# Seven block products for the keys and queries of seven head pairs, on normalized input

## The chip, the cores and the metric

The kernel runs on one core of a Trainium2 chip. The metric is the device time of one execution in microseconds (us): the median of several runs. TensorE (PE) multiplies, VectorE (DVE), ScalarE (ACT) and GpSimd (POOL) work elementwise, SyncE (SP) issues most transfers.

## What is computed

One step of a small encoder trunk: 512 prompt frames and 8 streams of 16 sample frames, 640 columns in all, 1024 features. A convolution module and an FFN come first, then one attention layer with an FFN, then a final norm. The change lies in the attention layer:

```python
k, v = jnp.split(rms_norm(h, norm_kv) @ w_kv, 2, axis=-1)
q = (rms_norm(h, norm_attn[j]) @ w_q[j]).reshape(B, T, N_HEADS, HEAD_DIM)
...
o = band_attention_prompt(q, k, v, rel_bias[j])
h = h + o @ w_o[j]
```

`rms_norm` divides a frame by its root mean square and multiplies by a gain per feature. There are 16 heads of 64, worked on as 8 pairs; the prompt attends within itself, the samples to 512 cached rows and their own.

## The kernel before

Features lie on partitions (8 tiles of 128), frames on the free axis. Every matrix product is made in three: each operand is split into a high part (a rounded copy, made by ScalarE) and a low part (the rest, a subtraction on VectorE), and high x high, low x high and high x low are added up in PSUM. So a weight tile costs a ScalarE and a VectorE operation before TensorE may use it.

The stage begins where the first layer's FFN ends. The FFN's last products are made for group 0 (256 columns) and then for group 1 (384 columns), eight output tiles each, and VectorE adds them into h (L705).

`rms_late` (L314) splits the raw h for each group (L190, L192) and works out 1/rms beside that: squares on ScalarE (L211), their sum over the eight tiles (L233), a product with a column of ones on TensorE for the mean (L243), epsilon on VectorE (L280), the power on Pool (L287) and a product that spreads the result over the partitions (L257). The row of 1/rms is used only at the eviction of a projection: L1228 and L1310 multiply keys and queries by it, L1251 and L1338 the values. The gains are multiplied into the weights when these are split: L167 and L168 (`wsplit`) for pair 0, L1290 and L1291 (`pieces`) for the others, in 16 pieces of 128 columns.

`run(proj_kq(0), proj_v(0))` makes the first pair's keys and queries and the first values: keys and queries of group 0, values of group 0, then the same of group 1. After that comes the loop over the pairs. A pair's attention is the steps A (scores of two heads, row maxima, exponentials, normalisation), S (sample scores), B and T (transposes), C (products with the values), written in `BO`. Between the steps, portions f of other products fill TensorE: `stream()` yields the projections of later pairs (k), values (v) and output products (o) in the order of `SETS`, and `FILL` says how many portions a pair takes. In `set_kq` (L1296) a pair's keys and queries are four results (two groups, two kinds) of 8 x 3 matmuls each, of 256 or 384 columns. The weights of the next set are split while the current set runs, in whole tiles of 2048 columns with two buffers. `samp_load` fetches a pair's cached keys and values when the pair begins.

A scheduler puts the instructions in the order of each engine, and each engine works through its own in that order. `high_priority` moves instructions ahead, `behind` and `issue_after` hold them back.

Of the kernel before, what the change touches and what calls it, by code (L numbers as in the profile page):

```python
# [8 lines left out]
F32 = mybir.dt.float32  # L9
# [6 lines left out]
P = 128  # L16
# [49 lines left out]
BO = ["A f4 S w f4 B f3 T f3 C f*"] * 8  # L66
BO[1] = BO[6] = "A f4 S w f5 B f5 T f5 C"
BO[7] = "A f2 S f2 w f4 B f3 T f3 C f*"
FILL = 20, 19, 28, 27, 28, 20, 19, 16
SETS = "k1 v1 k2 k3 o0 k4 v2 k5 o1 k6 v3 k7 o2"  # L70
# [15 lines left out]
def tile_trunk(ctx, tc, xT, vecs, hist, w_pw1, w_pw2, w_in0, w_out0, w_os0, w_in1, w_out1, w_os1,  # L86
# [227 lines left out]
    def rms_late(g, gain, engs=SQ, cut=CUT):  # L314
        n = gr[g][1]
        xh, xl = new_xs(g)
        for k in range(KT):
            src = hp(g, k)
            if gain is not None:
                t = tp.tile([P, tw[0]], F32, tag="n1", name=nm("n1"), bufs=NB1)  # L320
                nc.vector.tensor_scalar(out=t[:, :n], in0=src, scalar1=col(gain, k),
                                        scalar2=None, op0=ALU.mult)
                src = t[:, :n]
# [787 lines left out]
    tps, early = ExitStack(), ExitStack()  # L1111
    op_ = early.enter_context(tc.tile_pool(name="op", bufs=1, reuse_waits="tile"))
    xp = early.enter_context(tc.tile_pool(name="xp1", bufs=1, reuse_waits="tile"))
    w2 = early.enter_context(tc.tile_pool(name="w2c", bufs=2, space=PSUM, reuse_waits="tile"))
    mm = tps.enter_context(tc.tile_pool(name="mm3", bufs=4, space=PSUM, reuse_waits="tile"))
    tp = tps.enter_context(tc.tile_pool(name="tp2", bufs=2, reuse_waits="tile"))

    xs = [rms_late(0, None), rms_late(1, None)]
    tps.close()
    at = ExitStack()  # L1120
    am = at.enter_context(tc.tile_pool(name="am", bufs=2, space=PSUM))
    mm = at.enter_context(tc.tile_pool(name="mm1", bufs=2, space=PSUM))
# [173 lines left out]
    def set_kq(p, w):  # L1296
# [4 lines left out]
        for g, (g0, n) in enumerate(GR):  # L1301
            for t, dst in enumerate((kt, qt)):
                pt = mmt()
                for a, b in zip(PARTS, PARTS[1:]):
# [3 lines left out]
                    if b == KT:  # L1308
# [9 lines left out]
                        if g and t:  # L1318
                            nc.sync.dma_start(k_out[p], kt)
                            split[p] = heads_split(p)  # L1320
# [516 lines left out]
```

## Time and profile before

| | |
|---|---|
| median of 3 runs | 1445.13 us (1444.21 to 1446.97) |
| the profiled execution | 1444.19 us |
| its span | 1442.4 us |
| TensorE busy | 1419.1 us, 98% |
| VectorE, ScalarE, Pool busy | 77%, 52%, 20% |
| the FFN's last product ends, first projection begins | 663.8, 664.7 us |
| first attention step | 692.2 us |
| data moved | 192.57 MB, mean 134 GB/s |

The profile is one execution. A busy share says how full an engine is, not whether something waits for it; here TensorE is full nearly everywhere, and the question at each place is which other engine it would wait for. A row of the timeline has start, duration, engine, line, operation, output<-inputs and count; in brackets stands the idle time before it and what ended it. Durations of matmuls overlap.

### The profile page before, as it was taken

Reading aid. Unit: us, or ns where it says so; the run is one execution under the profiler, and the core shown is the slowest. Engines: PE = TensorE matmul, PEld = TensorE weight load, DVE = VectorE, ACT = ScalarE, POOL = GpSimd, SP = SyncE. Lnnn points to the kernel's source line nnn. Section 1 sums busy time; section 2 is a strip of 40 time slices with the busy share of each in tenths; the row PEclk is TensorE's granted clock in tenths of the full one; section 3 lists DMA queues with packets and bytes.
Section 4 is the critical chain, followed back from the end, with each engine's and each line's share of the span. In section 5 each row is a group of like instructions: output and inputs, shape, how many; then the busy total and the mean of one; then the engine's idle time right before and its main releaser. Section 6 shows DMA issues by size and latency. Waiting matters only on the chain. (4 is left out here: it accounts for less than half of the span.)

```text
span 1442.4 us, 28233 instructions
## 1 busy us (share of the span) xinstructions
PE 1419.1 (98%) x11086; PEld 1366.2 (95%) x11086; DVE 1114.5 (77%) x2474; ACT 746.0 (52%) x1617; POOL 282.9 (20%) x335
## 2 busy tenths in 40 slices
PE   9999999999999999999999999998999999999998
PEld 8998799999999999999998999988999999999998
DVE  6789867898788789766666757667898788888855
ACT  5666554564554554545654544534564554554443
POOL 5789121011111111012111111110011111111101
PEclk9999999999999999999999999999999999999999
DMA  7267424054534445424456455561034544444512
GB/s 246 74 185 182 131 81 143 13 142 125 156 95 141 132 116 127 139 88 172 164 185 219 166 179 183 182 207 60 30 106 123 160 113 121 130 119 124 148 59 74
DMA packets 66932, 192.57 MB, mean 134 GB/s; under 512 B 12144, under 2 KB 30320, under 8 KB 58480
## 3 DMA queue, kind: packets, MB, share of 16 engines
q1 hardware_dynamic: 52432, 160.58, 34.0%
q0 software_dynamic: 13504, 29.37, 10.2%
q8 instruction: 87, 1.43, 0.4%
q10 hardware_dynamic: 864, 0.83, 0.2%
q14 instruction: 45, 0.37, 0.1%
HBM read 179.14 MB, written 11.61 MB: 132 GB/s over the span
## 5 line engine op out<-in xcount | busy, mean ns | idle before, releaser
L442 PE MATMUL mm<-XH,whi 128*128 128x320 f32 x896 | 275.7, 310 | 2.6 <-ACT t L454 2.6
L442 PE MATMUL mm<-XH,wlo 128*128 128x320 f32 x896 | 276.1, 309 | 0.0
L442 PE MATMUL mm<-XL,whi 128*128 128x320 f32 x896 | 274.5, 309 | 0.0
L374 ACT ACTIVATE whi<-raw 128x512 fp32r<-128x512 f32 (+2 forms) x280 | 168.8, 613 | 136.0 <-PE mm L442 105.5
L375 DVE TENSOR_TENSOR wlo<-raw,whi 128x512 fp32r<-128x512 f32 (+2 forms) x280 | 184.2, 666 | 17.4 <-ACT whi L374 16.2
L442 PE MATMUL mm<-hid,whi 128*128 128x320 f32 x732 | 171.8, 310 | 3.0 <-DVE hid L375 2.2
L442 PEld LDWEIGHTS mm<-XH,whi 128*128 128x128 f32 x896 | 167.7, 188 | 4.2 <-ACT t L454 4.2
L442 PEld LDWEIGHTS mm<-XH,wlo 128*128 128x128 f32 x896 | 168.1, 188 | 0.0
L442 PEld LDWEIGHTS mm<-XL,whi 128*128 128x128 f32 x896 | 167.7, 188 | 0.0
L442 PEld LDWEIGHTS mm<-hid,whi 128*128 128x128 f32 x732 | 124.8, 188 | 5.5 <-DVE hid L375 3.2
L202 PE MATMUL mm<-xh,whi 128*128 128x320 f32 (+2 forms) x416 | 129.0, 312 | 0.8 <-DVE h L705 0.4
L203 PE MATMUL mm<-xh,wlo 128*128 128x320 f32 (+2 forms) x416 | 127.9, 309 | 0.0
L204 PE MATMUL mm<-xl,whi 128*128 128x320 f32 (+2 forms) x416 | 125.8, 310 | 0.0
L442 PE MATMUL mm<-hid,wlo 128*128 128x320 f32 x366 | 113.0, 309 | 0.0
L442 PE MATMUL mm<-XH,shi 128*128 128x320 f32 x344 | 105.9, 309 | 0.7 <-DVE h L1552 0.7
L442 PE MATMUL mm<-XH,slo 128*128 128x320 f32 x344 | 106.0, 308 | 0.0
L442 PE MATMUL mm<-XL,shi 128*128 128x320 f32 x344 | 105.5, 308 | 0.0
L420 POOL DMA_DIRECT2D s<-in_w_in x38 | 22.1, 581 | 372.7 <-DVE wlo L375 147.7
L844 POOL TENSOR_TENSOR ca<-ca,cvt 128x512 f32<-128x512 f32 x60 | 91.8, 1530 | 16.4 <-ACT cvt L841 9.9
L374 ACT ACTIVATE shi<-raw 128x512 fp32r<-128x512 f32 (+1 forms) x114 | 66.7, 588 | 44.7 <-PE mm L442 41.2
L454 ACT ACTIVATE t<-mm 128x320 f32<-128x320 f32 x114 | 49.5, 434 | 64.5 <-PE mm L442 64.2
L583 DVE TENSOR_TENSOR h<-h,mm 128x320 f32<-128x320 f32 x168 | 79.6, 479 | 2.9 <-PE mm L442 2.8
(330 smaller groups left out, 3673.7 us busy)
## 6 DMA issues: line engine op xcount, KB each, us to landing
raw<-in_w_in SPq DMA_DIRECT2D x38, 1024.0 KB
s<-in_w_in POOLq DMA_DIRECT2D x76, 256.0 KB, 4.1
raw<-in_w_os SPq DMA_DIRECT2D x24, 768.0 KB
cache<-in_ck SPq DMA_DIRECT2D x32, 512.0 KB
cache<-in_cv SPq DMA_DIRECT2D x32, 512.0 KB
raw<-in_w_pw SPq DMA_DIRECT2D x11, 1024.0 KB
s<-in_w_os POOLq DMA_DIRECT2D x48, 192.0 KB, 3.6
raw<-in_w_kq SPq DMA_DIRECT2D x8, 1024.0 KB
```

The costliest lines, as they stand in the source:

```text
L202: nc.tensor.matmul(ps, wh, xh, start=(first and i == 0), stop=False)
L203: nc.tensor.matmul(ps, wl, xh, start=False, stop=False)
L204: end = nc.tensor.matmul(ps, wh, xl, start=False, stop=(stop and i == last))
L374: put_end[1] = nc.scalar.activation(out=hi, in_=src, func=AF.Copy).ins
L375: put_end[0] = nc.vector.tensor_tensor(out=lo, in0=src, in1=hi.bitcast(F32), op=sub).ins
L420: nc.gpsimd.dma_start(s1, src[:, 2 * n:3 * n])
L442: last = nc.tensor.matmul(pt, wt, v, start=(first and k == i == 0), stop=(k == n - 1 and i == 2), skip_group_check=True)
L454: keeps.append(nc.scalar.activation(out=t, in_=pt, func=AF.Copy).ins)
L583: nc.vector.tensor_tensor(out=hv, in0=hv, in1=pt, op=sub if row else add)
L844: nc.gpsimd.tensor_tensor(out=acc, in0=acc, in1=pr, op=ALU.add)
```

## The change

- **Seven products.** The keys and queries of pairs 1 to 7 are a product of a 2 x 2 block matrix of weights (keys and queries by two halves of the features) with a 2 x 2 block matrix of input (halves of the features by halves of the columns). It is made with seven block products of 4 x 3 matmuls of 320 columns instead of eight. The block sums of the input (`xsum`, four with high and low parts) are made once by VectorE and ScalarE, those of the weights for each pair by VectorE. The seven products alternate between two PSUM banks and are evicted by copies on ScalarE and additions on VectorE.
- **Normalized input.** The sums need input that has been divided by its rms. `rms_kept` (in place of `rms_late`) works out 1/rms first, multiplies h by it on VectorE (L324 of the new kernel) and splits the product (L192, L194). The evictions become plain copies. The squares lie in two tiles, the sum in a third, for both groups.
- **Gains.** For keys and queries ScalarE multiplies the raw weights by the gains in place, 16 pieces of 128 columns, and the blocks are then added and split in seven pieces of 512 columns.
- **A ring.** Split weights lie in six slots of 512 columns; `advance` makes pieces up to nine portions ahead, if a slot is free. Raw weights come in quarters into one buffer. The second buffers of before hold cached keys and values now, which are fetched in two steps: values after S, the next pair's keys after C.
- **Order.** `SETS`, `BO` and `FILL` are new: v1 comes before k1, and a keys-and-queries set has 14 portions of 6 matmuls instead of 12 of 6 or 9. The scores, transposes and products of the attention are as before.

```diff
-SETS = "k1 v1 k2 k3 o0 k4 v2 k5 o1 k6 v3 k7 o2"
-FILL = 20, 19, 28, 27, 28, 20, 19, 16
+FILL = 29, 21, 26, 26, 24, 24, 25, 16
+LEAD = 9
+RING = 6
+SETS = "v1 k1 k2 v2 k3 o0 k4 k5 o1 k6 v3 k7 o2 o3"
...
-    def rms_late(g, gain, engs=SQ, cut=CUT):
-        n = gr[g][1]
-        xh, xl = new_xs(g)
-        for k in range(KT):
-            src = hp(g, k)
...
-            xsplit(src, xh[:, k, :], xl[:, k, :])
-        rt = cst.tile([P, 4], F32, tag=f"rt{g}", name=nm("rt"))
+    def rms_kept(g, x, rows, sqs, acc):
+        g0, n = gr[g]
+        xh, xl = (t[:, :, g0:g0 + n] for t in x)
         with tc.high_priority(offset=HP):
-            bc, _ = rstd_bc([hp(g, k) for k in range(KT)], n, engs, cut, rt,
-                            nc.vector if g else nc.gpsimd)
-        b = xp.tile([P, n], F32, tag=f"bc{g}", name=nm("bc"))
-        nc.scalar.activation(out=b, in_=bc, func=AF.Copy)
-        return xh, xl, b, rt
+            bc, _ = rstd_bc([hp(g, k) for k in range(KT)], n, SQ, CUT, None, nc.vector, accp=acc,
+                            sqs=sqs)
+            for k in range(KT):
+                t = rows[k][:, g0:g0 + n]
+                nc.vector.tensor_tensor(out=t, in0=hp(g, k), in1=bc, op=ALU.mult)
+                xsplit(t, xh[:, k, :], xl[:, k, :])
+        return xh, xl
...
-    xs = [rms_late(0, None), rms_late(1, None)]
+    for g in range(2):
+        q = [kept[:, i, :gr[g][1]] for i in range(3)]
+        xs.append(rms_kept(g, xall, rows, (q[0], q[1]) * 4, q[2]))
...
-                nc.vector.tensor_tensor(out=dst[:, g0:g0 + n], in0=pt[:, :n], in1=xs[g][2],
-                                        op=ALU.mult)
+                nc.vector.tensor_copy(dst[:, g0:g0 + n], pt[:, :n])
...
+        for op in "0 e 1 f 2 3 s a b c d g - -".split():
+            yield op in "efabcdg"
+            with behind(*past[-LAG].values()):
+                if op in "0123":
+                    for k in range(4):
+                        c = 4 * int(op) + k
+                        sl = rawt[:, c * P:c * P + P]
+                        nc.scalar.activation(out=sl, in_=sl, func=AF.Copy, scale=gkq[:, c:c + 1])
+                elif op == "e":
+                    put(a11)
...
+                elif op == "s":
+                    add(s1, a21, a22)
+                    add(a21, a11, a21)
+                elif op == "a":
+                    add(a11, s1, a11)
+                    put(a11)
...
+    def advance(n=2, lead=None):
+        for _ in range(n):
+            if given[0] >= spent[0] + (lead or LEAD):
+                return
+            if wants[0] and taken[0] - freed[0] == RING:
+                return
+            wants[0] = next(pieces, False)
+            given[0] += 1
...
+        def end(i):
+            if i == 0:
+                note(copy(out=k0, in_=pa, func=AF.Copy))
+            elif i == 1:
+                note(add(out=k0, in0=pb, in1=k0, op=ALU.add))
...
+        for i, (pt, x, w, done) in enumerate(((pa, X11, 0, 1), (pb, X21, 1, 1), (pa, XT2, 2, 1),
+                                              (pb, XT1, 3, 1), (pa, XT3, 4, 1), (pb, X22, 5, 1),
+                                              (pa, XT4, 6, 1))):
+            hi, lo = ws[w]
+            for a in (0, 2):
+                part(pt, [(hi[:, k * P:k * P + P], lo[:, k * P:k * P + P]) for k in (a, a + 1)],
+                     [(xsum[x][0][:, k, :], xsum[x][1][:, k, :]) for k in (a, a + 1)],
+                     a == 0 and i in (0, 1, 3), a == 2)
...
+    with behind(*put_last):
+        for k in range(4):
+            (n11, n12), (n21, n22) = ((r[:, 0:NH], r[:, NH:]) for r in (rows[k], rows[k + 4]))
+            nc.vector.tensor_tensor(out=n11, in0=n11, in1=n12, op=ALU.subtract)
+            nc.vector.tensor_tensor(out=n12, in0=n22, in1=n12, op=ALU.subtract)
...
-        cache = [samp_load(p, u) for u in range(2)]
...
+            if op == "S":
+                values = load_v(p)
...
+            elif op == "C" and p + 1 < NP:
+                keys = load_k(p + 1)
...
-    w_kq = np.stack([wk, wq], axis=3).reshape(NP, P, 2048)
+    w_kq = np.stack([wk, wq], axis=2).reshape(NP, P, 2048)
```

The first place is the seam between the FFN and the first projection. VectorE before, from the last FFN addition into h (L705) on; xl is the low part of the input, wlo a low part of weights, acc the sum of squares, kt the keys of pair 0:

```order
L705 TENSOR_TENSOR h<-mm_7359,h 128x384
L192 TENSOR_TENSOR xl_7448<-h,xh_7447 128x384
L168 SCALAR_TENSOR_TENSOR wlo_7634<-raw_7632,vec,whi_7633 128x256 x2
L280 TENSOR_SCALAR rst_7440<-w_738_7413 128x2
L233 TENSOR_TENSOR acc_7469<-sq_7467,sq_7470 128x384
L168 SCALAR_TENSOR_TENSOR wlo_7634<-raw_7632,vec,whi_7633 128x256 x6
L192 TENSOR_TENSOR xl_7448<-h,xh_7447 128x384
L233 TENSOR_TENSOR acc_7469<-acc_7469,sq_7473 128x384
L1228 TENSOR_TENSOR kt_7576<-mm_7578,bc_7445 128x256
```

and now (L700 is the FFN's addition, xt_7406 holds squares and their sum, w_752 the spread 1/rms of group 0, row_7393 a tile of normalized input):

```order
L700 TENSOR_TENSOR h<-mm_7345,h 128x384
L700 TENSOR_TENSOR h<-mm_7359,h 128x384
L235 TENSOR_TENSOR xt_7406<-xt_7406 128x256
L170 SCALAR_TENSOR_TENSOR wlo_7640<-raw_7638,vec,whi_7639 128x256 x8
L235 TENSOR_TENSOR xt_7406<-xt_7406 128x256 x6
L235 TENSOR_TENSOR xt_7406<-xt_7406 128x384
L282 TENSOR_SCALAR rst_7426<-w_752_7408 128x2
L235 TENSOR_TENSOR xt_7406<-xt_7406 128x384 x5
L324 TENSOR_TENSOR row_7393<-h,w_752_7408 128x256
```

The raw input's split and the early key evictions are gone from here; the sum of group 0's squares, which Pool made, stands behind the last FFN addition, and the product with 1/rms behind group 1's sums. Further down the same row, at the end of the eight products of group 0:

```order
L324 TENSOR_TENSOR row_7399<-h,w_752_7408 128x256
L324 TENSOR_TENSOR xt_7407<-h,w_752_7408 128x256
L235 TENSOR_TENSOR xt_7406<-xt_7406 128x384
L194 TENSOR_TENSOR xl_7392<-row_7393,xh_7391 128x256
L194 TENSOR_TENSOR xl_7392<-row_7394,xh_7391 128x256
```

Group 1's seventh addition stands behind the last of these products. ScalarE at the same place, before (sq squares, xh high part of the input, whi_7541 high part of the first w_kq, whi_7633 of the first w_v):

```order
L190 ACTIVATE xh_7394<-h 128x256
L211 ACTIVATE sq_7435<-h 128x256
L190 ACTIVATE xh_7394<-h 128x256
L211 ACTIVATE sq_7467<-h 128x384
L190 ACTIVATE xh_7447<-h 128x384
L211 ACTIVATE sq_7470<-h 128x384
L190 ACTIVATE xh_7447<-h 128x384 x2
L167 ACTIVATE whi_7541<-raw_7540,vec 128x128 x12
L190 ACTIVATE xh_7447<-h 128x384
L167 ACTIVATE whi_7541<-raw_7540,vec 128x128 x4
L190 ACTIVATE xh_7447<-h 128x384 x3
L167 ACTIVATE whi_7633<-raw_7632,vec 128x256 x8
```

and now (whi_7549 is w_kq, whi_7639 w_v):

```order
L369 ACTIVATE hid_6611<-t_714_7075 128x320
L169 ACTIVATE whi_7549<-raw_7548,vec 128x128 x16
L213 ACTIVATE xt_7406<-h 128x256 x2
L169 ACTIVATE whi_7639<-raw_7638,vec 128x256 x8
L213 ACTIVATE xt_7406<-h 128x256 x6
L213 ACTIVATE xt_7406<-h 128x384 x8
L192 ACTIVATE xh_7391<-row_7393 128x256
```

Six of group 0's eight squares moved behind the eight pieces of w_v. TensorE there, before (mm_7359 is the FFN's last product, w_738 the mean of group 0):

```order
L204 MATMUL mm_7359<-hid_6612,whi_2832 128x384
L243 MATMUL w_738_7413<-onec,acc_7416 128x1 x2
L202 MATMUL mm_7578<-xh_7394,whi_7541 128x256
L203 MATMUL mm_7578<-xh_7394,wlo_7542 128x256
L204 MATMUL mm_7578<-xl_7395,whi_7541 128x256
```

and now (w_752 mean and spread of group 0, w_755 mean of group 1, mm_7513 and mm_7512 the two banks):

```order
L206 MATMUL mm_7359<-hid_6612,whi_2832 128x384
L245 MATMUL w_752_7408<-onec,xt_7406 128x1 x2
L259 MATMUL w_752_7408<-ident,rst_754_7428 128x128 x2
L204 MATMUL mm_7513<-xh_7391,whi_7549 128x256
L205 MATMUL mm_7513<-xh_7391,wlo_7550 128x256
L204 MATMUL mm_7512<-xh_7391,whi_7549 128x256
L205 MATMUL mm_7512<-xh_7391,wlo_7550 128x256
L245 MATMUL w_755_7456<-onec,xt_7406 128x1 x3
L206 MATMUL mm_7513<-xl_7392,whi_7549 128x256
```

The spread moved ahead of the first projection, and group 1's mean into it, after four matmuls.

The second place is ScalarE in pair 1, around the exponentials of the two heads (S), before (whi_8239 high parts of the next keys and queries, vt_8227 an eviction of values):

```order
L1290 ACTIVATE whi_8239<-raw_8238,vec 128x128 x3
L1194 ACTIVATE S_8428,sm_8430<-S_8428,nb_8435 128x512
L1194 ACTIVATE S_8428,sm_8430<-S_8428,nb_8435 128x384
L1194 ACTIVATE S_8428,sm_8430<-S_8428,nb_8435 128x128
L1194 ACTIVATE S_8428,sm_8430<-S_8428,nb_8435 128x256
L1194 ACTIVATE S_8447,sm_8449<-S_8447,nb_8454 128x512
L1194 ACTIVATE S_8447,sm_8449<-S_8447,nb_8454 128x384
L1338 ACTIVATE vt_8227<-mm_8475,rt_7465 128x256
L1194 ACTIVATE S_8447,sm_8449<-S_8447,nb_8454 128x128
L1194 ACTIVATE S_8447,sm_8449<-S_8447,nb_8454 128x256
L1194 ACTIVATE Sn,sm_8517<-Sn,nb_8519 128x576
L1194 ACTIVATE Ss_8533,sm_8535<-Ss_8533,nb_8537 128x576
```

and now (kt_8549 the keys of pair 2, raw_7836 the raw weights, whi_7838 and wlo_7840 slots of the ring):

```order
L1421 ACTIVATE kt_8549<-mm_7513 128x320
L1291 ACTIVATE wlo_7840<-raw_7836 128x512
L1206 ACTIVATE S_8510,sm_8512<-S_8510,nb_8517 128x512
L1206 ACTIVATE S_8510,sm_8512<-S_8510,nb_8517 128x384
L1206 ACTIVATE S_8510,sm_8512<-S_8510,nb_8517 128x128
L1206 ACTIVATE S_8510,sm_8512<-S_8510,nb_8517 128x256
L1206 ACTIVATE S_8529,sm_8531<-S_8529,nb_8536 128x512
L1206 ACTIVATE S_8529,sm_8531<-S_8529,nb_8536 128x384
L1206 ACTIVATE S_8529,sm_8531<-S_8529,nb_8536 128x128
L1206 ACTIVATE S_8529,sm_8531<-S_8529,nb_8536 128x256
L1291 ACTIVATE whi_7838<-raw_7836 128x512
L1425 ACTIVATE kt_8549<-mm_7513 128x320
```

A 512-column piece and an eviction of pair 2's keys stand behind the eight exponentials now, where small pieces stood before and after them.

More of the change, by code (lines that the diff above doesn't have):

```diff
@@ L1364, in stream, with o_part @@
[L1364 to L1388 removed]
+    def o_part(pt, r, ws, m, g0):
+        c = slice((m % 2) * P, (m % 2) * P + P)
+        part(pt, [[t.rearrange("p (k c) -> p k c", k=2)[:, k, c] for t in ws[m // 2]]
+                  for k in range(2)],
+             [[t[:, g0:g0 + NH] for t in oT[2 * r + k]] for k in range(2)], True, True)
@@ L1590, in tile_trunk @@
                 elif op == "S":
-                    sa = [samp_a(p, u, w2t(), *cache[u]) for u in range(2)]
+                    sa = [samp_a(p, u, w2t(), keys[u]) for u in range(2)]
                 elif op == "B":
```

381 lines of the change are left out of this document (230 added, 151 removed).

## The prediction, made before the changed kernel ran

> **What bounds the kernel now.** I read the page first, then the time by stages, then TensorE's rows.
>
> ```profile
> span 1442.4 us, 28233 instructions
> PE 1419.1 (98%) x11086; PEld 1366.2 (95%) x11086; DVE 1114.5 (77%) x2474; ACT 746.0 (52%) x1617; POOL 282.9 (20%) x335
> ```
>
> TensorE (PE) is busy all the time. The windows (busy time of PE, PEld, DVE, ACT, POOL; then clock, DMA share, GB/s) show the changed stage: first the projections of pair 0, then the attention loop.
>
> ```profile
> 664.70:697.30 32.60, 32.60 (x256) 32.20 (x257) 18.65 (x56) 14.55 (x38) 9.10 (x18) 1.00 0.61 226
> 697.30:985.00 287.70, 285.04 (x2764) 255.93 (x2763) 185.25 (x574) 138.59 (x391) 44.96 (x81) 1.00 0.55 182
> ```
>
> In 320 us TensorE lacks work for 2.7 us. So fewer matmuls are worth their full time here, and every new wait of TensorE costs its full time. A matmul's price is its distance to the next one, since durations overlap: PE rows of 256 and 384 columns, first and last of 33 and of 9, and one piece of the chain with 703 of 320.
>
> ```profile
> 697.30 0.28 PE L1272 MATMUL mm<-xh,whi 128*128 128x256 f32 x1
> ...
> 701.14 0.28 PE L1272 MATMUL mm<-xl,whi 128*128 128x256 f32 x1
> 701.35 1.06 PE L1482 MATMUL w<-cache,qbd 128*32 128x512 f32 x8
> ...
> 703.43 0.39 PE L1272 MATMUL mm<-xh,whi 128*128 128x256 f32 x1
> ...
> 705.33 0.34 PE L1272 MATMUL mm<-xh,whi 128*128 128x384 f32 x1
> ...
> 706.72 0.33 PE L1272 MATMUL mm<-xl,whi 128*128 128x384 f32 x1
> ```
>
> ```profile
> 1097.39 103.67 PE mm L442 x703
> ```
>
> That is 3.84/32 = 0.120 us, 1.39/8 = 0.174 us and 103.67/703 = 0.1475 us. (The sample scores between, 701.35 to 703.43, take 2.1 us; they come back below.)
>
> **Seven products.** A pair's keys and queries take 48 matmuls of 256 and 48 of 384 columns: 5.76 + 8.35 = 14.1 us. Seven block products take 7 x 4 x 3 = 84 of 320: 12.4 us. Seven pairs save 7 x 1.72 = **12.0 us**. Values, output products and attention keep their matmuls.
>
> **The norm moves in front of the projections.** Before, raw h was split and projected, and 1/rms was multiplied in at the eviction. PE rows at the seam, and the first product of the values:
>
> ```profile
> 663.78 0.50 PE L243 MATMUL w<-onec,acc 128*128 128x1 f32 x4
> 664.68 0.36 PE L202 MATMUL mm<-xh,whi 128*128 128x256 f32 x1 [0.40 <-DVE h L705]
> ```
>
> ```profile
> L202 PE MATMUL mm<-whi,xh x40: 278/283/387, 670.9 to 696.9; 128*128 128x256 f32 x40
> ```
>
> TensorE waited 0.4 us. Now the first projection needs squares, sum, power, spread, product and split of group 0. The new order decides when. ScalarE's row has six of group 0's squares behind the eight pieces of the first w_v, whose buffer the last FFN product still reads; VectorE's row has the sums of squares behind the last FFN addition. ScalarE's and VectorE's rows of before give the durations.
>
> ```profile
> 663.98 3.31 ACT L167 ACTIVATE whi<-raw,vec 128x256 fp32r<-128x256 f32 x8
> ```
>
> ```profile
> 640.20 1.08 DVE L705 TENSOR_TENSOR h<-mm,h 128x256 f32<-128x256 f32 x3
> ...
> 663.98 0.56 DVE L705 TENSOR_TENSOR h<-mm,h 128x384 f32<-128x384 f32 x1
> 664.45 0.55 DVE L192 TENSOR_TENSOR xl<-h,xh 128x384 fp32r<-128x384 f32 x1
> ...
> 669.99 1.21 DVE L233 TENSOR_TENSOR acc<-acc,sq 128x384 f32<-128x384 f32 x2
> ...
> 671.49 1.87 DVE L233 TENSOR_TENSOR acc<-acc,sq 128x384 f32<-128x384 f32 x3
> ```
>
> From mean to spread I take the kernel's later norm (PE, then DVE):
>
> ```profile
> 998.18 0.83 PE L1625 MATMUL w<-onec,sqs 128*128 128x1 f32 x6 [1.57 <-DVE sqs L1618]
> ...
> 1001.14 0.93 PE L257 MATMUL w<-ident,sqs 128*128 128x128 f32 x6 [0.26 <-POOL sqs L1629]
> ```
>
> ```profile
> 999.05 0.16 DVE L1627 TENSOR_SCALAR sqs<-w 128x3 f32<-128x3 f32 x1 [0.32 <-PE w L1625]
> ```
>
> The chain, on the clock of before, with the last FFN product over at 663.8:
> - w_v's pieces, 3.3 us: 667.2. Six squares, each waiting for an addition to free one of two buffers: (673.36 - 669.99)/5 = 0.67 us a round at 384 columns; between 0.45 (by columns) and 0.67 I take 0.5: 670.3.
> - Mean to spread 1001.14 - 998.18 = 2.96 us; the epsilon stands behind group 1's first addition, 0.7 more: 674.0, and 0.4 of spread. VectorE has five more additions of group 1 ahead of the products, 5 x 0.67 = 3.4 us from 671.8: 675.2, later than the spread. So 675.2.
> - Eight products h x 1/rms at 0.36 us: 678.1. TensorE gets four matmuls at about 675.9, and then its row has group 1's mean, which waits for the seventh addition behind those eight products: 678.6, and 0.5: **679.1**. Of 15.3 us TensorE has worked 1.9 (two means, a spread, four matmuls); less the old 0.4, 13.0 us are new.
> - The second wait. Group 1's epsilon stands behind eight low parts (2.9 us): 681.5; to the spread 1001.14 - 999.05 = 2.1 us: 683.6. TensorE has 29 matmuls (3.5 us) before it and waits 1.0 us. After it come 0.5 us of spread and 15 matmuls, to 685.9; the values' first product needs the bank that VectorE empties only behind eight products of 384 columns (664.45 - 663.98 = 0.47 each) and a copy of 0.42: 688.3, 2.4 us of wait.
>
> Together **16.4 us**. Cross-check: the values' first product moves from 670.9 to 688.3, 17.4 us, of which 1.0 is group 1's mean and spread, which stood behind it. Bounds: 13 (shorter rounds, a spread that is ready at once) and 18 (if the first two squares wait for the FFN too, 0.8 more, and a slow Pool).
>
> **A restart from idle.** The longest waits of TensorE in the trace are these, the second of them at the very start:
>
> ```profile
> PE mm L149 <- POOL ident masks.py:199: 1.6, 1, 1.6
> PE w L1625 <- DVE sqs L1618: 1.6, 1, 1.6
> ```
>
> So no gap like the new one is there to read. At the start, TensorE comes from rest and repeats one 128-column matmul (windows of line 149 alone):
>
> ```profile
> 3.00:5.00 2.00, 2.00 (x12) 2.00 (x10) 1.00 1.06 386
> 5.00:7.00 2.00, 2.00 (x11) 2.00 (x11) 1.00 1.04 354
> 7.00:9.00 2.00, 2.00 (x18) 2.00 (x18) 1.00 0.97 351
> ```
>
> Some 11.5 in 2 us, then 18, with the granted clock shown as 1.00 throughout: by that column nothing is lost, by the counts a rested TensorE runs 1.57 times slower. If 13 us rest it, the 29 matmuls take 2.0 us more, of which the spread's 1.0 us wait hides half. I take 1.0, bounds 0 and 1.5. The Trainium skill, "TensorE: Matmul & The Clock Gate", Part 1, speaks against this change: after an idle window of about 3.4 us the array runs at half rate until it was busy for as long. By it, as an estimate, 1.7 us would be lost and 0.7 left after the wait, and the sum 0.3 us lower; no run here shows it behind such a gap.
>
> **Weights and evictions in the loop.** A pair's pieces cost ScalarE 16 scalings and 7 copies where it had 16 multiplying copies, VectorE 7 subtractions and 4 additions for 16, and evictions come every 1.77 us. By group, one piece of 512 columns (ACT, DVE):
>
> ```profile
> L374 ACT ACTIVATE whi<-raw 128x512 fp32r<-128x512 f32 x162 | 100.4, 628 | 56.8 <-PE mm L442 43.3 <-DVE raw L428 8.1 <-DVE h L583 2.0
> L375 DVE TENSOR_TENSOR wlo<-raw,whi 128x512 fp32r<-128x512 f32 x162 | 109.9, 684 | 7.1 <-ACT whi L374 6.5
> ```
>
> So ScalarE gets some 4 + 2 us more a pair and VectorE 2 to 3, beside 40 us of TensorE: free on average. But the rows are in order. ScalarE's exponentials, then VectorE's row maxima and normalisation:
>
> ```profile
> 735.44 0.72 ACT L1194 ACTIVATE S<-S,nb 128x512 f32<-128x512 f32 x1 [1.00 <-DVE nb L1191]
> ...
> 740.17 0.76 ACT L1194 ACTIVATE Sn<-Sn,nb 128x576 f32<-128x576 f32 x1
> ...
> 741.69 0.98 ACT L1290 ACTIVATE whi<-raw,vec 128x128 fp32r<-128x128 f32 x3
> ...
> 744.64 2.15 ACT L1290 ACTIVATE whi<-raw,vec 128x128 fp32r<-128x128 f32 x7
> ```
>
> ```profile
> 694.15 0.69 DVE L1202 CUSTOM_DVE_ANT_0 S<-w,BP 128x512 f32<-128x512 f32 x1 [1.64 <-PE w L1416]
> ...
> 697.45 0.28 DVE L1191 TENSOR_SCALAR nb<-mx 128x4 f32<-128x4 f32 x2
> ```
>
> ```profile
> 772.34 1.51 DVE L1432 TENSOR_SCALAR S<-S,rs 128x512 f32<-128x512 f32 x4
> 773.77 0.74 DVE L1202 CUSTOM_DVE_ANT_0 Ss<-w,BS 128x576 f32<-128x576 f32 x1
> ```
>
> The maxima hold VectorE for 3.4 us, eight exponentials (735.44 to 740.17) ScalarE for 4.7, all ten (to 741.69) for 6.3, one scaling of 128 columns 2.15/7 = 0.31. In pair 1 the fifth block's piece stands behind eight exponentials, which end 3.4 + 4.7 = 8.1 us after the scores; its low part stands behind one head's normalisation (1.5) and a sample's maxima (0.7) as well and takes 0.7: 11.0. TensorE wants it after eight portions of 6 x 0.1475 us and the sample scores: 7.1 + 2.1 = 9.2. So some 2 us of wait. In pair 0 VectorE has the block sums too: by the order, 7 of their operations of 0.4 us stand among the maxima, and by the chain above the maxima start some 1.7 us late, so the exponentials start at 1.7 + 3.4 + 2.8 = 7.9 us. ScalarE has ten of them, 12 scalings, two more evictions (0.9) and a piece (0.6) before TensorE's first block product: 7.9 + 6.3 + 3.7 + 0.9 + 0.6 = 19.4, and 0.7 for the low part, 20.1. TensorE's cover is the values' 120 x 0.120 us, the sample scores and 0.6 of transposes: 17.1. So some 3 us. Elsewhere the same rows fit by a few tenths. An estimate of two such chains is soft: I take **4 us** for the 5 and all the rest, bounds 0 and 12 (2 us in six pairs). Below zero only the 2.7 us that TensorE lacks now could be won; nothing in the change touches those places.
>
> **Sum** against the profiled execution (1444.2 us, span 1442.4 and 1.8 around it; the median of the runs is 1445.13): 1444.2 - 12.0 + 16.4 + 1.0 + 4 = 1453.6, say **1453.5 us**.
>
> **The rivals.**
> - *The forecast, 0.55:* the seam costs more than seven products save; 1448.1 to 1458.
> - *The ring decides, 0.15:* weights come late in six pairs, not two; 8 us more than taken: 1458 to 1465. For: six slots hold less than one set of seven. Against: VectorE is busy for 64% of the loop and ScalarE for 48%.
> - *The seam at its low bound and a loop without waits, 0.13:* 1444.2 - 12.0 + 13 + 0 to 2.5 = 1445 to 1448, no change that a measurement can tell.
> - *Faster, 0.17:* group 0's 1/rms is ready under the last FFN products, as it nearly was before. It decides if the six squares come ahead of w_v's pieces. Then only the first product and split (1.5 us), the second wait (3.4) and 2 us in the loop are left: 1444.2 - 12.0 + 6.9 = 1439. For: group 0's residual is complete 15 us before the FFN ends. Against: the order of both rows.
>
> That the change doesn't save the matmuls is no rival: the order shows 336 of 256 and 336 of 384 columns less and 588 of 320 more.
>
> **How the numbers follow.** A measurement can tell about 0.2%, 2.9 us. Slower by more: 0.55 + 0.15 = 0.70; within: 0.13; faster: 0.17. The range leaves out most of the last case and the end of the second: 1441 to 1462. The likeliest case alone: 1448 to 1458.
>
> **What would show it.** Right: a gap of TensorE of 11 to 13 us between the last FFN addition and the key products, ended by VectorE's sum of squares; a second of about 2 us before the values, ended by the copy of the keys; 84 matmuls of 320 columns a pair, at 0.1475 us. In the loop, waits of 2 to 3 us for low parts of pieces in pairs 0 and 1. Wrong: a seam gap under 8 us, or loop waits above 12 us.

## The result and the profile after

The changed kernel takes 1515.0 us (median of 4 runs, 1510.1 to 1517.0), the kernel before 1445.8: 1.0474 times as long, 95% interval 1.0447 to 1.0502. Slower was forecast, by 8 us; it is 69. The profiled execution took 1515.89 us, with this page:

```profile
span 1514.1 us, 28238 instructions
PE 1440.0 (95%) x11002; PEld 1378.5 (91%) x11002; DVE 1149.2 (76%) x2484; ACT 785.8 (52%) x1699; POOL 281.8 (19%) x330
PEclk9999999999999999988999999899999999999999
```

The 84 matmuls fewer are there (11086 to 11002), TensorE is no longer full, and the granted clock (PEclk), full throughout before, dips in the 18th, 19th and 26th slices (at the seam and in the loop).

The windows of both kernels over three stages (PE, PEld, DVE, ACT, POOL busy; clock, DMA share, GB/s): seam up to the first scores, loop from the first to the last scores, and from there to the next FFN. Before:

```profile
663.80:692.20 28.40, 28.00 (x213) 27.84 (x211) 16.02 (x43) 14.90 (x39) 9.79 (x20) 1.00 0.60 226
692.20:957.70 265.50, 264.44 (x2549) 239.29 (x2550) 171.68 (x536) 130.10 (x367) 41.92 (x77) 1.00 0.57 189
957.70:1005.00 47.30, 43.21 (x383) 37.97 (x379) 34.62 (x93) 18.94 (x46) 4.76 (x5) 1.00 0.34 106
```

After:

```profile
666.50:719.60 53.10, 34.95 (x212) 33.98 (x212) 31.21 (x75) 22.92 (x54) 9.33 (x20) 0.74 0.24 75
719.60:1025.30 305.70, 274.95 (x2465) 242.85 (x2466) 192.74 (x519) 167.60 (x448) 47.55 (x77) 0.94 0.50 161
1025.30:1074.80 49.50, 43.68 (x383) 38.32 (x379) 37.90 (x98) 22.32 (x53) 3.88 (x5) 1.00 0.42 130
```

The span grew by 71.7 us: 2.7 before the seam (code that the change doesn't touch; the clock was 0.50 from 30.4 to 33.8 us, which takes 1.7 of them), 24.7 at the seam, **40.2 in the loop**, 4.1 behind it. The rest before the seam and what lies behind the loop have no cause shown here. At the seam 17.4 were forecast. The loop, which was to shrink by 12.0 and lose 4, is where the forecast broke.

TensorE's rows at the seam (start, duration, what; in brackets the wait):

```profile
673.76 0.98 PE L245 MATMUL w<-onec,xt 128*128 128x1 f32 x4 [7.31 <-DVE xt L235]
681.11 1.22 PE L259 MATMUL w<-ident,rst 128*128 128x128 f32 x4 [6.36 <-POOL rst L289]
683.29 0.58 PE L204 MATMUL mm<-xh,whi 128*128 128x256 f32 x1 [0.96 <-ACT xh L192]
...
698.04 0.38 PE L204 MATMUL mm<-whi,xh 128*128 128x256 f32 x1 [2.44 <-DVE kt L1240]
```

The wait for the sum of squares (7.31) was forecast, and so was the one for the copy of the keys (2.44). The 6.36 us for Pool's power were not. Pool's row:

```profile
672.61 2.65 POOL L1173 TENSOR_SCALAR BP<-BP,t 128x256 f32<-128x256 f32 x2 [4.33 <-DMA BP<-in_rel]
...
678.54 0.34 POOL L1188 TENSOR_SCALAR BS<-bt,t256s 32x16 f32<-32x16 f32 x1 [2.13 <-DMA bt<-in_rel]
...
680.33 0.72 POOL L289 TENSOR_TENSOR rst<-rst,mhalf 128x2 f32<-128x2 f32 x1
```

The power has no wait in brackets: it simply stands behind the first pair's bias operations, two of which wait for transfers.

TensorE's waits in the loop (total, times, longest):

```profile
PE mm L1406 <- DVE wlo L1292: 13.2, 9, 2.2
PE mm L1406 <- ACT wlo L1291: 6.5, 4, 2.9
PE mm L1406 <- DVE h L1495: 3.9, 2, 2.3
PE mm L1406 <- ACT qt L1434: 3.1, 1, 3.1
```

All rows of that answer come to 30.7 us, where before there was one wait of 1.0. Most, 20.0 us, end with a weight piece (L1291, L1292). They lie in every pair: 3.7, 5.4, 3.7, 4.7, 4.1, 6.0 and 2.9 us from one pair's scores to the next. And they cost more than their length. Two windows at the first of them, which ends at 745.8 us:

```profile
744.00:748.00 4.00, 1.39 (x5) 1.16 (x6) 3.52 (x7) 2.87 (x7) 0.00 (x0) 0.90 0.41 140
748.00:752.00 4.00, 4.00 (x21) 4.00 (x20) 2.77 (x6) 2.11 (x4) 0.00 (x0) 0.67 0.43 132
```

From 748 to 752 us TensorE is busy throughout and the clock is 0.67. Added up over the loop in windows of 4 us, busy time times what the clock lacks of 1.00, that is **16.2 us** lost after the waits; in the loop before it is 0.0. At the seam the same sum is 6.9 us, and there too 0.0 before.

### The profile page after: what moved, and what is told of

It reads as the page before. It is cut to its first block, busy times and chain, and to the rows that moved or that the text cites. A ratio compares the mean times of both kernels' runs of the same rounds, so it can differ in the third digit from the quotient of the medians.

```text
span 1514.1 us, 28238 instructions
## 1 busy us (share of the span) xinstructions
PE 1440.0 (95%) x11002; PEld 1378.5 (91%) x11002; DVE 1149.2 (76%) x2484; ACT 785.8 (52%) x1699; POOL 281.8 (19%) x330
## 4 chain that ended last, share of the span: by engine, by line
PE 72%; DVE 15%; ACT 6%; DMA 4%; issue 2%; POOL 1%; DVEq 0%; SPq 0%; POOLq 0%; ACTq 0%
PE mm L437 42%; PE mm L204 5%; PE mm L206 5%; PE mm L205 5%; PE mm L1406 5%; PE mm L883 2%; DMA raw<-in_w_os 2%; ACT raw L1328 1%; DVE wlo L370 1%; PE w L1554 1%; DVE wlo L1292 1%; DVE S L1214 1%; DMA raw<-in_w_in 1%; ACT S L1206 1%; PE am L1640 1%
## 5 line engine op out<-in xcount | busy, mean ns | idle before, releaser
L204 PEld LDWEIGHTS mm<-xh,whi 128*128 128x128 f32 x416 | 79.9, 192 | 4.1 <-ACT xh L192 2.8
```

The lines of the kernel that those rows point to most:

```text
L204: nc.tensor.matmul(ps, wh, xh, start=(first and i == 0), stop=False)
```

## Experiments

Theory: two of the change's parts lose time independently. At the seam the power waits in Pool's row; in the loop weights come too late in every pair, and the waits bring a slow clock as well. Rivals: the normalized input itself is what costs, at the seam or in the loop; or the seven products do not save what they should. Loop means first to last scores; its waits are the sum of TensorE's, and "clock" is the sum described above. The last three columns and the first scores come from one profiled execution of each kernel. `loads_early`, `gains_left_out`, `lead_loads` and `supply_bound` leave out work that the result needs, and serve as bounds only.

| kernel | us | ratio to before (95%) | first scores at | loop | waits | clock |
|---|---|---|---|---|---|---|
| before | 1445.8 | | 692.2 | 265.5 | 1.0 | 0.0 |
| after | 1515.0 | 1.0474 (1.0447 to 1.0502) | 719.6 | 305.7 | 30.7 | 16.2 |
| norm_alone | 1452.1 | 1.0041 (1.0026 to 1.0056) | 699.6 | 265.4 | 1.0 | 0.0 |
| pool_first | 1504.5 | 1.0401 (1.0386 to 1.0417) | 709.9 | 302.1 | 31.4 | 11.6 |
| loads_early | 1497.9 | 1.0367 (1.0343 to 1.0392) | 708.2 | 291.3 | 29.0 | 2.8 |
| gains_left_out | 1480.7 | 1.0235 (1.0220 to 1.0251) | 709.0 | 280.0 | 17.9 | 4.4 |
| lead_14 | 1479.3 | 1.0230 (1.0212 to 1.0248) | 708.7 | 281.8 | 18.5 | 6.3 |
| gains_on_pool | 1479.1 | 1.0230 (1.0209 to 1.0250) | 708.5 | 281.2 | 20.0 | 4.6 |
| lead_loads | 1473.8 | 1.0194 (1.0177 to 1.0211) | 707.8 | 273.9 | 13.4 | 3.2 |
| supply_bound | 1463.5 | 1.0118 (1.0103 to 1.0134) | 710.0 | 265.1 | 8.2 | 1.7 |

### The norm alone

`norm_alone` is the kernel before with `rms_front` for `rms_late`, plain evictions, and the bias operations behind the powers:

```diff
+    def rms_front(g):
...
+            bc, _ = rstd_bc([hp(g, k) for k in range(KT)], n, SQ, CUT, None, nc.vector)
+            for k in range(KT):
+                t = tp.tile([P, tw[0]], F32, tag="n1", name=nm("n1"), bufs=NB1)[:, :n]
+                nc.vector.tensor_tensor(out=t, in0=hp(g, k), in1=bc, op=ALU.mult)
+                xsplit(t, xh[:, k, :], xl[:, k, :])
...
-    xs = [rms_late(0, None), rms_late(1, None)]
+    xs = [rms_front(0), rms_front(1)]
...
-                nc.vector.tensor_tensor(out=dst[:, g0:g0 + n], in0=pt[:, :n], in1=xs[g][2],
-                                        op=ALU.mult)
+                nc.vector.tensor_copy(dst[:, g0:g0 + n], pt[:, :n])
...
-    bias_load(0)
+    bias_load(0, norm_end["pow"])
```

> The kernel before with one part of the change alone: input normalized in front of all projections (squares, sum, power, spread, then multiply and split), plain evictions, the old eight products, old weights, old order; Pool's bias operations held behind the powers. Theory (two losses): the norm in front costs the seam alone, 16 to 22 us, so 1462 to 1468, the loop from first to last scores stays 265 to 267 us without waits, and the other 50 us of the changed kernel belong to the seven products and their weights. Rival (the input normalized first is what holds the loop too, by its evictions or by memory): 1480 to 1515. Rival (my sum for the seam, with Pool out of the way): 1461 to 1463.

The loop stayed at 265.4 us, so normalized input is not what holds it. The seam cost far less than either sum of mine: first scores 7.4 us later, 5.9 us on the ratio. TensorE's rows:

```profile
667.24 1.08 PE L257 MATMUL w<-ident,rst 128*128 128x128 f32 x4 [2.68 <-POOL rst L287]
669.98 0.58 PE L202 MATMUL mm<-xh,whi 128*128 128x256 f32 x1 [1.66 <-ACT xh L190]
```

ScalarE's rows show why: here the squares of group 0 run beside the FFN's last products.

```profile
640.98 0.71 ACT L211 ACTIVATE sq<-h 128x256 f32<-128x256 f32 x2
...
648.14 0.42 ACT L211 ACTIVATE sq<-h 128x256 f32<-128x256 f32 x1 [0.99 <-DVE h L716]
```

### The seam

`pool_first` is the changed kernel with Pool's first bias operations behind the powers:

```diff
-    bias_load(0)
+    bias_load(0, norm_end["pow"])
...
-    def bias_load(p):
+    def bias_load(p, *tie):
+      with behind(*tie):
```

> The changed kernel with one thing mended: the first pair's bias operations on Pool are held behind the two powers of the norm. Theory (Pool's row): group 0's 1/rms was late because the power stood behind bias operations that waited for a transfer, 5.0 us (675.33 to 680.33); with them behind, the spread starts about 1.2 us after the mean instead of 6.4, and the time falls by 4 to 6 us to about 1510; the loop stays as it is. Rival (the chain of squares and sums sets the seam, Pool only fills the time): within 1 us of 1515. A third way: the bias arrives later and the first attention step waits for it, 1513 to 1518.

It gained 10.6 us, twice what I expected. TensorE's rows:

```profile
672.66 0.98 PE L245 MATMUL w<-onec,xt 128*128 128x1 f32 x4 [7.23 <-DVE xt L235]
675.23 1.22 PE L259 MATMUL w<-ident,rst 128*128 128x128 f32 x4 [1.59 <-POOL rst L289]
677.70 0.58 PE L204 MATMUL mm<-xh,whi 128*128 128x256 f32 x1 [1.24 <-ACT xh L192]
```

The wait for Pool went from 6.36 to 1.59. The first scores moved by 9.7 us, of which 1.0 lies before the seam (the FFN's last product ends at 665.4 instead of 666.5) and 8.7 at it. The theory holds for Pool's row. That the gain is twice the forecast is not its doing alone: the loop, with the same waits, lost 4.6 us less to the clock and was 3.6 shorter.

`squares_first` adds tiles of their own for squares and sum, and the first pair's weight splits behind the squares:

```diff
+    tps = ExitStack()
+    tq = tps.enter_context(tc.tile_pool(name="tq", bufs=2, reuse_waits="tile"))
...
+        sq_last = sq_last if g else norm_end["sq"]
...
+        with behind(sq_last):
+            wh, wl = wsplit(w_kq[p], 16, P, gains=GKQ)
```

> The kernel with Pool mended (1504.45) and, in addition, group 0's squares in front of the split of the first pair's weights on ScalarE, with the squares and their sum in tiles of their own. Theory (order on ScalarE): the mean of group 0 came 7.2 us late because two squares ran before and six behind the eight pieces of the values' weights; in front of them they lie beside the FFN's last products, as in the run with the norm alone, where the spread came at 667.2 and the first scores at 699.6 against 709.9: 7 to 10 us off, 1494 to 1498. Rival (the squares wait for memory that the FFN's last products still read): they stay behind 663 us, and less than 2 us is gained.

1512.1 us (1.0451, 1.0435 to 1.0466), slower than `pool_first`, so the theory on ScalarE's order fell. The first scores came at 713.2, 3.3 us later; the loop was 5.2 longer, 5.0 of them by the clock (16.6 against 11.6). ScalarE's rows:

```profile
640.87 0.47 ACT L369 ACTIVATE hid<-t 128x320 fp32r<-128x320 f32 x1 [1.33 <-DVE t L477]
664.53 0.72 ACT L213 ACTIVATE sq<-h 128x256 f32<-128x256 f32 x2 [23.19 <-PE mm L206]
```

The first square now stands at the head of ScalarE's row and still waits 23.19 us for an FFN product, though it reads only h. That points to its tile, which takes room that the FFN still reads, as the rival had it; this is argued from the wait, not tried with other addresses. The weight splits, now behind the squares, stand ahead of the splits of normalized input instead, and TensorE waited 4.9 us for the first of these.

Does the slow clock hold the seam? `pool_first_warm` and `warm_short` put products that nothing reads into the two waits (60 + 12, and 27 + 6):

```diff
+        if keep:
+            for i in range(27):
+                nc.tensor.matmul(st[:, 768:896], keep, ident, start=True, stop=True)
```

> The same, and 60 + 12 products of 128 columns that nothing reads keep TensorE busy between the FFN's last product and the spread of group 0 (before the mean and between mean and spread). Theory (the clock): after the seam the granted clock was 0.50 to 0.67 until 704 us in the changed kernel, and some 6 us of the 27 that the first attention step comes later are that; kept busy, the matmuls behind the spread run at 0.12 us from the start, and the time is 4 to 6 us under the run with Pool mended, about 1505. Rival (the slow matmuls behind the seam wait for the splits of the normalized input, not for a clock): no change, about 1510, with pitches still near 0.25 us. If the filler is too long it moves the mean, and the time is above.

1515.9 us (1.0479, 1.0455 to 1.0502). The filler took 13.66 us and moved the mean to 679.0; as a test of the clock it is void.

> Pool mended and a filler of the right length: in the run with 60 + 12 products the filler took 13.66 and 2.94 us (0.23 us each) and moved the mean from 672.7 to 679.0, so its time told nothing. Now 27 before the mean (6.1 us in a wait of 7.2) and 6 between mean and spread (1.4 us in 1.6). Theory (the clock): with Pool mended the clock was 0.50 from 674 to 686 us, and 6 us of that were full of matmuls, so 3 us there and 1 us in mean and spread are the slow clock: 3 to 4.5 us off, 1500 to 1501.5, first scores at 705.5 to 707 instead of 709.9. Rival (the splits of the normalized input set the pace there, the slow matmuls only fill the waits): within 1.5 us of 1504.4, first scores after 708.4.

1511.1 us (1.0443, 1.0425 to 1.0460), first scores at 711.6: not the theory. The filler fits, and TensorE's row shows what it runs into:

```profile
665.58 6.29 PE L280 MATMUL w<-ident,h 128*128 128x128 f32 x54 [0.65 <-DVE h L707]
672.06 0.61 PE L245 MATMUL w<-onec,xt 128*128 128x1 f32 x4 [0.19 <-DVE xt L235]
...
677.96 0.39 PE L204 MATMUL mm<-xh,whi 128*128 128x256 f32 x1 [2.46 <-ACT xh L192]
```

```profile
676.00:680.00 4.00, 1.51 (x10) 1.28 (x10) 3.90 (x11) 3.01 (x9) 0.00 (x0) 1.00 0.21 79
680.00:684.00 4.00, 3.36 (x15) 3.36 (x16) 3.00 (x10) 0.70 (x3) 2.50 (x2) 0.50 0.00 0
```

The clock stays at 1.00 until 680 us, yet the first product starts no earlier, since it waits for the split; TensorE is then busy for only 1.51 of 4 us, and the clock falls anyway. The loop behind it, with the same rows, took 307.9 us against 302.1, 4.1 of the 5.8 by the clock (15.7 against 11.6). So the loop's loss changes by some 5 us though its code does not.

### The clock after a wait

`forced_gaps` is the kernel before with seven waits put into TensorE's row:

```diff
+            nc.tensor.matmul(g[:, 0:1], ident, onec, start=True, stop=True)
+            nc.vector.tensor_copy(lag_t[:, 0:1], g[:, 0:1])
+            for i in range(n):
+                a, b = (0, 256) if i % 2 == 0 else (256, 0)
+                nc.vector.tensor_copy(lag_t[:, b:b + 256], lag_t[:, a:a + 256])
```

> The kernel before with seven gaps forced into TensorE's row, one in each of the pairs 0 to 6: a small product, 1, 2, 4, 6, 8, 10 and 12 small copies in a row on VectorE, and a small product that reads the last. Idle times of about 0.6, 0.9, 1.5, 2.2, 2.8, 3.5 and 4.1 us are aimed at, 15 to 16 us in all. Theory A (short waits slow the clock too): gaps over about 2 us are followed by 3 to 4 us at half rate, about 1.7 us lost for each of four, in all 1467 to 1469. Theory B (only idle time over 3.4 us does): two of them, 1463 to 1465. Theory C (no gap changes the rate): 1460 to 1462.

1484.6 us in its one run. The waits came out longer than aimed at, 1.45 to 4.92 us and 23.3 together, and the span grew by 40.4. The first four of them in TensorE's rows:

```profile
713.59 0.38 PE L1569 MATMUL am<-onec,lag 128*128 128x1 f32 x2 [1.45 <-DVE lag L1564]
752.37 0.38 PE L1569 MATMUL am<-onec,lag 128*128 128x1 f32 x2 [2.33 <-DVE lag L1567]
790.04 0.38 PE L1569 MATMUL am<-onec,lag 128*128 128x1 f32 x2 [2.60 <-DVE lag L1567]
835.08 0.59 PE L1569 MATMUL am<-onec,lag 128*128 128x1 f32 x2 [3.38 <-DVE lag L1567]
```

The windows right behind each:

```profile
713.60:717.60 4.00, 4.00 (x15) 4.00 (x16) 0.92 (x2) 0.13 (x1) 0.00 (x0) 0.57 0.48 117
752.40:756.00 3.60, 3.60 (x29) 3.60 (x30) 0.16 (x1) 0.00 (x0) 0.00 (x0) 1.00 0.88 309
790.00:794.00 4.00, 3.96 (x25) 3.93 (x26) 0.00 (x0) 0.00 (x0) 0.00 (x0) 1.00 0.83 283
835.00:839.00 4.00, 3.92 (x13) 3.92 (x14) 0.03 (x1) 0.00 (x0) 0.00 (x0) 0.50 0.81 285
```

Every wait from 3.38 us on is followed by a clock of 0.50 to 0.58 for the next 4 us; those of 2.33 and 2.60 us are not; that of 1.45 us is. So none of the three theories holds as a rule on length. The four waits of 3.38 us and more each brought a slow phase; of the three shorter ones one did. The Trainium skill ("TensorE: Matmul & The Clock Gate", Part 1) says that the gate judges by windows of about 3.4 us that run freely, so what counts is how a wait falls into them. The traces bear this out: read in steps of 0.1 us, the slow phases of `forced_gaps` begin at 714.14, 833.61, 881.40, 929.18 and 973.56 us, which are 35, 14, 14 and 13 steps of 3.413 us apart, and each lasts one or two steps.

Cut at such marks, taken for each kernel from its own slow phases, the loops show what the waits have in common. Two windows of the changed kernel, each with the one behind it:

```profile
743.82:747.23 3.41, 0.62 (x2) 0.39 (x3) 2.94 (x6) 3.05 (x8) 0.00 (x0) 1.00 0.27 87
747.23:750.64 3.41, 3.41 (x14) 3.41 (x14) 2.75 (x5) 1.05 (x3) 0.00 (x0) 0.50 0.46 146
...
921.31:924.72 3.41, 1.75 (x14) 1.25 (x12) 1.37 (x3) 0.95 (x2) 0.00 (x0) 1.00 0.67 196
924.72:928.14 3.42, 2.91 (x21) 2.65 (x22) 1.99 (x5) 1.25 (x3) 0.00 (x0) 1.00 0.04 16
```

Busy for 0.18 of the first, TensorE got half the clock in the next; busy for 0.51, it kept the full one. The loops of the changed kernel and its ten variants have 860 such windows at full clock. All 43 with a busy share under 0.47 are followed by a slow one, none of the 803 from 0.51 up, and 8 of the 14 between. In `forced_gaps` the three short waits do not sort this way (a share of 0.57 was followed by a slow window, 0.52 and 0.47 were not), so the busy share is not the whole of it; the one-column products around its waits count as busy.

### The loop

All of these start from `pool_first`. `lead_14` changes one number:

```diff
-LEAD = 9
+LEAD = 14
```

> The kernel with Pool mended and LEAD 14 in place of 9: weight pieces may be made fourteen portions ahead, as far as six slots allow. Theory (too short a lead): the 26 to 30 us of waits in the loop are pieces that were asked for too late; with the longer lead half of them go, with the slow clock behind them, 1480 to 1492. Rival (the two engines' rows: a piece stands behind the scores' additions and exponentials whenever it was asked for, and the six slots are full anyway): within 3 us of 1504.

25 us gained, 0.7 more than the theory's best: it holds. TensorE's waits in its loop:

```profile
PE mm L1407 <- DVE h L1496: 4.5, 2, 2.9
PE am L1533 <- DVE olo L194: 3.1, 1, 3.1
PE mm L1407 <- ACT kt L1426: 2.4, 1, 2.4
PE mm L1407 <- ACT qt L1435: 2.0, 1, 2.0
...
PE mm L1407 <- DVE wlo L1293: 0.3, 1, 0.3
```

The waits for pieces went from some 20 us to 0.5. What is left are evictions and additions behind other work, one kind of which ScalarE's row shows:

```profile
774.13 0.91 ACT L1295 ACTIVATE whi<-raw,vec 128x256 fp32r<-128x256 f32 x2 [1.11 <-DMA raw<-in_w_v]
774.94 0.42 ACT L1435 ACTIVATE qt<-mm 128x320 f32<-128x320 f32 x1
```

The eviction stands behind a piece whose load has not landed; in the changed kernel the same eviction held TensorE for 3.1 us.

`gains_left_out` takes the in-place scalings away:

```diff
-                    for k in range(4):
-                        c = 4 * int(op) + k
-                        sl = rawt[:, c * P:c * P + P]
-                        nc.scalar.activation(out=sl, in_=sl, func=AF.Copy, scale=gkq[:, c:c + 1])
+                    pass
```

> The kernel with Pool mended, and the gains of the keys' and queries' weights of the pairs 1 to 7 left out (16 in-place multiplications on ScalarE for each set, some 0.29 us each, 4.7 us a set, 33 us in all). Theory (ScalarE's work on the supply): the first pieces of a set come 4 to 5 us earlier, and the waits for splits fall by half or more: 1480 to 1492. Rival (VectorE's additions and subtractions and its row set the pace): within 4 us of 1504.

24 us gained as well, as the theory had it, though the waits fell a little less than by half (31.4 to 17.9): with 32 us less on ScalarE, the old lead nearly does. `gains_on_pool` tried to have that with LEAD 14 and nothing left out:

```diff
-                        nc.scalar.activation(out=sl, in_=sl, func=AF.Copy, scale=gkq[:, c:c + 1])
+                        nc.gpsimd.tensor_scalar(out=sl, in0=sl, scalar1=gkq[:, c:c + 1],
+                                                scalar2=None, op0=ALU.mult)
```

> Pool mended and LEAD 14, and the in-place gains done by Pool instead of ScalarE, nothing left out. Theory (ScalarE's row was the tight one, Pool has room): 1466 to 1474. Rival (Pool's own row: a gain stands behind a bias operation that waits for a transfer, and costs 0.9 us instead of 0.29): pieces come later, 1485 to 1510.

No gain over `lead_14` and no loss: neither reading holds. One wait of 6.6 us for a sum of queries took the place of others; its cause stays open.

`loads_early` gives each set of raw weights a buffer, and `lead_loads` is that with LEAD 14:

```diff
-        for t, nxt in zip(todo, todo[1:] + [None]):
+        for i, (t, nxt) in enumerate(zip(todo, todo[1:] + [None])):
             stock[t] = []
+            cur[0] = raws[i % 2]
+            for q in range(4 if nxt else 0):
+                fetch(nxt, q, raws[(i + 1) % 2])
```

> The kernel with Pool mended and two raw weight buffers, each set loaded whole while the set before is split; the room comes from cached keys and values, which are loaded once for the first pair and read again by the others (left out: their later loads). Theory (the loads): quarters that are fetched only when the last reader of a quarter is done hold the pieces up, as at 792.5 us, where the eviction stood 3.1 us behind pieces of values whose load took 5.2 us: the sum of waits falls by a third, 1490 to 1497. Rival (loads matter in that one place and one more): 3 to 7 us, 1497 to 1501. If it does nothing, 1503 to 1506.

> Pool mended, LEAD 14 and the early loads together (two raw buffers, cached keys and values loaded once; left out: their later loads). With LEAD 14 alone (1479.3) what is left in the loop are evictions on ScalarE that stand behind pieces whose load is under way (1.5, 2.0 and 2.4 us) and additions into h behind the scores. Theory (the lead and the loads act one after the other): the three evictions go with their slow clock, 1470 to 1474. Rival (they overlap; other waits take their place): 1477 to 1480. Both would be untouched by the seam, first scores at 708 to 710.

6.5 us alone (1497.9), between the theory's range and the rival's end. The waits only fell from 31.4 to 29.0; the rest is the clock, 11.6 to 2.8 in the profiled execution. That one took 1493.1 us, the fastest of four that went up to 1503.3 with the granted clock falling from 0.989 to 0.980, so the 2.8 is probably its low end. And leaving out the later loads lightens the queues too (DMA share of the loop 0.51 to 0.24); no run separates that from loading early. On top of LEAD 14 another 5.5, at the edge of the theory: the three evictions' waits went, and of the 13.4 us left only 1.6 end with a weight piece.

`supply_bound` has all three, LEAD 14, early loads and no scalings:

> The same with the gains of the keys' and queries' weights left out as well (and the later loads of cached keys and values), so that the supply of weights is as light as this layout allows. Theory (seven products save what the matmul pitches say, 12 us, once nothing is waited for): from first to last scores 254 to 262 us instead of 265.6 before and 305 after, and 1458 to 1466. Rival (the order of the portions itself makes waits: additions into h and evictions stand behind the scores' work on VectorE whatever the weights do): the loop stays over 270 us, and the time over 1470.

Its loop and what it still waits for:

```profile
710.00:975.10 265.10, 256.52 (x2463) 228.43 (x2464) 193.94 (x522) 138.38 (x339) 45.61 (x77) 0.99 0.27 82
```

```profile
PE mm L1412 <- DVE h L1501: 4.3, 2, 2.7
PE w L1560 <- DVE S L1573: 1.4, 1, 1.4
PE w L1412 <- DVE h L1501: 1.2, 1, 1.2
```

The time is where the theory had it, the loop 3 us above it. Of 265.1 us, 8.2 are waits and 1.7 slow clock: 255.2 are left, against 264.5 before (265.5 less 1.0). So the seven products do save time, 9.3 us of the 12.0, and even with the lightest supply the waits that are left give it back. Nearly all of these end with additions into h or a copy of transposed scores, both on VectorE, not with a piece. That the order of the portions makes them, as the rival had it, is argued from these rows; no other order was tried.

Among the variants of the changed kernel that leave nothing out, the best took 1479.1 us. None beats the kernel before.

## Why the prediction was wrong

- **Seven products**, -12.0 us: right in kind. 84 matmuls fewer are on the page, and `supply_bound` shows 9.3 us of it. In the changed kernel itself the same sum, the loop less waits and slow clock, leaves 258.8 us, 5.7 less than before; what takes the other 6.3 stays open.
- **The norm moves in front of the projections**, +16.4 us: the chain up to the first key product was right, one row was missing. With Pool mended that product comes 12.3 us after the FFN's end (677.7), forecast 12.1 (675.9). The values' first product, at 688.9 us with 688.3 forecast, is in part luck: the two waits worked out ahead of it (1.0 and 2.4 us) did not come in `pool_first`, and products at half clock filled the time. The step that failed is "From mean to spread I take the kernel's later norm": it took the power as free to run, and looked at ScalarE's and VectorE's new order but not at Pool's, where the bias operations had moved ahead of it. That cost 8.7 us at the seam, and 10.6 in all came back with Pool mended. That the norm must cost 16 us was also more than the idea asks: alone, with squares that run beside the FFN's last products, it costs 7.4 at the seam.
- **A restart from idle**, +1.0, bounds 0 to 1.5: the mechanism was there, its size and count were not. It was priced as one restart behind one gap. At the seam TensorE's waits kept the clock at 0.50 from 668.7 to 692.6 us, and 6.9 us were lost; in the loop short waits bring it again and again, 16.2 us. The price came from the kernel's start, where the clock column shows 1.00; the trace's record of the clock begins only at 7.5 us, so that 1.00 was no reading.
- **Weights and evictions in the loop**, +4, bounds 0 to 12: this is the term that was mis-sized, by 30.7 us of waits and the 16.2 behind them. The two chains that I worked out came about as forecast: 2.95 and 0.84 us in pair 0 (forecast 3), 1.98 in pair 1 (forecast 2). What failed is "Elsewhere the same rows fit by a few tenths", which was said of rows that I had not added up. Every pair waits 3 to 6 us, and the loop waits passed the 12 us that were named as proof against the forecast.
- **The rival "The ring decides"** had the mechanism, at 0.15, with 8 us more than the 4; it was 42 more (29.7 us of waits above those of before and 16.2 of slow clock, less the 4), of which 20.0 are waits for pieces. Its "against", VectorE busy 64% and ScalarE 48%, was read from the loop before, and says nothing: `lead_14` leaves both as busy as in `pool_first` (194 and 169 us of the loop, against 193 and 168) and gains 25 us. Pieces were late because they were begun late, then stood behind scores and exponentials, then held the next eviction. Six slots were enough once they were filled earlier.
- **The rival "Faster"** named squares ahead of the weight pieces as its point; `squares_first` shows that their order alone does not bring them under the FFN. `norm_alone`, where they lie there, took 1.0041 times the time of before, so even then the norm was no gain by itself.

## What to carry to other kernels

When a chain is moved in front of TensorE, go through the order of every engine that it touches, the idle ones too: Pool was 19% busy and its place in the row cost some 9 us. When an operand is made just in time through a ring, add up its chain for every round, not for two of them, and compare it with how far ahead it is begun; a busy share cannot show that it is late. And a wait on a TensorE that was full must be priced with the slow clock behind it, half as much again here: look at how busy it is left over 3.4 us, not at the length of one wait.

## What was not expected of the hardware

A wait of TensorE well under 3 us can halve its clock for the next microseconds: 1.45 us did in `forced_gaps`, 2.33 and 2.60 did not. The same loop, with 31 to 33 us of waits, lost 11.6, 15.7 or 16.2 us to it, depending on what stood in front. In the loops of eleven kernels the busy share of a window of 3.413 us tells which wait costs a slow one, with the edge between 0.47 and 0.51; what else counts in `forced_gaps` stays open. A filler of 128-column products in plain f32 took 0.23 us each at full clock (13.66 us for 60), and each counts as two in the rows (x120).
